# Squared distance from the row mean, one core: loads cut 3-3-2 rows, head loads and VectorE share removed

## Chip, cores and metric

One core of a Trainium2 chip. The metric is the device time in microseconds (us) of one execution. A profile's "span" is 1.7 to 1.8 us shorter than the time of its run. All runs below that are compared are in the fast state (granted clock 1.0 throughout); the single run that was not repeated is named.

## The reference

```python
x: float32, 1024 x 4096        # random normal
mean = np.mean(x, axis=-1, keepdims=True)
out  = (x - mean) ** 2         # float32, 1024 x 4096
```

16.78 MB are read and 16.78 MB written. Each of the 128 partitions of SBUF (the memory on the core) holds 8 rows of 4,096 elements; "row 3" below is the fourth row of every partition.

## The kernel before

Two tiles of four rows. Each tile's load has a small piece of 512 columns cut off ("head"), tile 0's on the SP queue (DMAs that SyncE issues), tile 1's on the ScalarE queue. VectorE makes the negated mean, ScalarE squares (x - mean) in place, and VectorE takes the last 512 columns of each tile's fourth row.

```python
for i in range(ntiles):                       # 2 tiles, Q = 4 rows, HEAD = 512
    x_tile = io.tile([P, Q * D], F32)
    if i == 0:
        nc.sync.dma_start(out=x_tile[:, :HEAD], in_=x_t[i][:, :HEAD])
        nc.sync.dma_start(out=x_tile[:, HEAD:], in_=x_t[i][:, HEAD:])
    else:
        end = Q * D - HEAD
        nc.scalar.dma_start(out=x_tile[:, end:], in_=x_t[i][:, end:])
        nc.sync.dma_start(out=x_tile[:, :end], in_=x_t[i][:, :end])
    ...
for i in range(ntiles):
    for q in range(Q):
        ...   # VectorE: neg_mean of the row (one tensor_tensor_reduce)
        cut = D if q < Q - 1 else LAST        # LAST = D - 512
        nc.scalar.activation(out=row[:, :cut], in_=row[:, :cut],
                             func=ACT.Square, bias=neg_mean, scale=1.0)
        if cut < D:
            ...   # VectorE: add neg_mean, multiply by itself, 512 columns
    nc.sync.dma_start(out=out_t[i], in_=tiles[i])
```

## Time and profile before

| | before |
|---|---|
| time, median of 3 runs | 82.99 us (82.96 to 82.99) |
| span of the profiled run | 81.4 us |
| DMA engines busy (both queues) | 96.1% of the span |
| ScalarE, VectorE busy | 36%, 26% |
| first store issued, second store issued | 39.73, 58.4 us |

A partition's share of one transfer is one piece, and each of the 16 DMA engines works through 8 pieces per transfer, one after the other. In the windows view a piece is booked where it begins, so the DMA share of a window of 1 us may be above 1. Two sums can be read from such a row. GB/s divided by share is the speed while busy. Share minus (GB/s / 434) is the time, in us of all 16 DMA engines, that the pieces begun there took beyond the plain rate of 434 GB/s. I call that the excess. The prediction shows the plain rate; the rows at the border of loads and stores, which it does not show, are these (columns: window, length, VectorE, ScalarE, GpSimd busy, clock, DMA share, GB/s):

```profile
38.00:39.00 1.00, 0.00 (x0) 1.00 (x1) 0.00 (x0) 1.00 2.05 889
39.00:40.00 1.00, 0.00 (x0) 0.71 (x1) 0.00 (x0) 1.00 0.29 127
40.00:41.00 1.00, 0.00 (x0) 0.00 (x0) 0.00 (x0) 1.00 0.15 66
41.00:42.00 1.00, 0.08 (x1) 0.00 (x0) 0.00 (x0) 1.00 2.30 983
```

889 / 2.05 = 434 for the last load pieces and 983 / 2.30 = 427 for the first store pieces: the kernel before passes from loading to storing without a loss worth the name.

### The profile page before, as it was taken

What the parts mean: (1) busy time and instruction counts of PE and PEld (TensorE: products, weight loads), DVE (VectorE), ACT (ScalarE), POOL (GpSimd) and SP (SyncE); (2) the same over time, 40 slices, a digit from 0 to 9 for tenths busy, and PEclk for the clock granted to TensorE, in tenths of its full rate; (3) what the DMA queues carried; (4) which work ended last, traced back from release to release, by engine and by line L of the source; (5) the groups of instructions that cost most, each with busy time, mean ns of one, the idle gap of its engine ahead of it and who ended that gap; (6) DMA issues with size and microseconds to landing.
All of it is one profiled execution on the core that took longest, in us unless ns stands there. A gap on an engine that the chain in (4) does not pass through costs nothing.

```text
span 81.4 us, 87 instructions
## 1 busy us (share of the span) xinstructions
DVE 20.8 (26%) x20; ACT 29.4 (36%) x9; POOL 0.2 (0%) x4
## 2 busy tenths in 40 slices
DVE  0000000000059999600039999700000000000000
ACT  0000000000054999999502999999600000000000
POOL 0000000000000000000000000000000000000000
DMA  1974999999759999995799993899996599999390
GB/s 22 704 343 187 499 499 499 499 499 437 343 218 499 499 499 499 499 406 250 343 516 515 515 515 161 354 515 515 515 516 290 258 483 515 515 515 419 161 451 0
DMA packets 864, 33.55 MB, mean 412 GB/s; under 512 B 96, under 2 KB 96, under 8 KB 352
## 3 DMA queue, kind: packets, MB, share of 16 engines
q1 hardware_dynamic: 720, 33.29, 95.0%
q10 hardware_dynamic: 144, 0.26, 1.1%
HBM read 16.78 MB, written 16.78 MB: 412 GB/s over the span
## 4 chain that ended last, share of the span: by engine, by line
DMA 49%; ACT 13%; ACTq 4%; DVE 3%; SPq 1%; issue 0%
DMA x_tile<-in_x_dram 49%; ACT x_tile L77 13%; ACTq L119 4%; DVE pairs L66 3%; SPq L53 1%; SPq L52 0%; DVE neg_mean L66 0%
## 5 line engine op out<-in xcount | busy, mean ns | idle before, releaser
L77 ACT ACTIVATE x_tile<-x_tile,neg_mean 128x4096 f32<-128x4096 f32 (+1 forms) x8 | 28.2, 3590 | 5.7 <-DVE neg_mean L66 5.7
L66 DVE CUSTOM_DVE_ANT_0 pairs<-x_tile 128x2048 f32<-128x2048 f32 x8 | 18.3, 2292 | 31.6 <-DMA x_tile<-in_x_dram 31.4
L77 ACT ACT_TABLE_LOAD x1 | 1.3, 1283 | 23.2 <-DMA x_tile<-in_x_dram 23.2
L87 DVE TENSOR_TENSOR x_tile<-x_tile 128x512 f32<-128x512 f32 x2 | 1.4, 692 | 0.1
L86 DVE TENSOR_SCALAR x_tile<-x_tile,neg_mean 128x512 f32<-128x512 f32 x2 | 1.0, 488 | 0.1
L66 DVE DVE_READ_ACCUMULATOR2_ANT neg_mean<- 128x1 f32 x8 | 0.7, 82 | 0.0
L105 POOL MEMSET const-bfloat16-1.0<- 128x1 bf16 x1 | 0.1, 102 | 0.0
L105 POOL MEMSET const-uint8-127<- 128x1 uint8 x1 | 0.1, 102 | 0.0
L105 POOL MEMSET const-float32-0.0<- 128x1 f32 x1 | 0.1, 99 | 0.2 <-issue 0.2
L105 POOL MEMSET const-float32-1.0<- 128x1 f32 x1 | 0.1, 99 | 0.0
## 6 DMA issues: line engine op xcount, KB each, us to landing
x_tile<-in_x_dram SPq DMA_DIRECT2D x2, 7936.0 KB, 31.1
x_tile<-in_x_dram ACTq DMA_DIRECT2D x1, 256.0 KB, 3.8
x_tile<-in_x_dram SPq DMA_DIRECT2D x1, 256.0 KB, 3.6
out_dram<-x_tile SPq DMA_DIRECT2D x2, 21.9
```

The source lines that it names most:

```text
L53: nc.sync.dma_start(out=x_tile[:, HEAD:], in_=x_t[i][:, HEAD:])
L66: inorder(nc.vector.tensor_tensor_reduce(out=pairs, in0=row[:, :HALF], in1=row[:, HALF:], scale=-inv_d, scalar=0.0, op0=ADD, op1=ADD, accu ...
L77: nc.scalar.activation(out=row[:, :cut], in_=row[:, :cut], func=ACT.Square, bias=neg_mean, scale=1.0,)
L86: nc.vector.tensor_scalar_add(out=rest, in0=rest, scalar1=neg_mean)
L87: nc.vector.tensor_mul(out=rest, in0=rest, in1=rest)
L105: nc = _bacc.Bacc("TRN2", target_bir_lowering=False, num_devices=1)
L119: with _tile.TileContext(nc) as tc:
```

## The change

The intent: fewer transfers and instructions, an earlier start of compute, an earlier first store. Loads of three, three and two rows, no heads, ScalarE squares whole rows, two stores of four rows. The diff is shortened. `load(lo, hi)` moves columns lo to hi of every partition's 8 rows on the SP queue, `store(first, last)` whole rows, `put(lo, hi)` stores by columns; `compute(r)` makes mean and square of row r; `inorder` keeps an instruction in program order.

```diff
-    # tiles of Q = 4 rows; heads of 512 columns on SP (tile 0) and ScalarE (tile 1)
-    nc.sync.dma_start(out=x_tile[:, :HEAD], ...)
-    nc.sync.dma_start(out=x_tile[:, HEAD:], ...)
-    nc.scalar.dma_start(out=x_tile[:, end:], ...)
-    nc.sync.dma_start(out=x_tile[:, :end], ...)
+    data = io.tile([P, ROWS * D], F32)          # one tile of 8 rows
+    load(0, 3 * D)                              # all on the SP queue
+    load(3 * D, 6 * D)
+    load(6 * D, 8 * D)
...
-            cut = D if q < Q - 1 else LAST
-            nc.scalar.activation(out=row[:, :cut], ...)
-            if cut < D:
-                nc.vector.tensor_scalar_add(out=rest, in0=rest, scalar1=neg_mean)
-                nc.vector.tensor_mul(out=rest, in0=rest, in1=rest)
-        nc.sync.dma_start(out=out_t[i], in_=tiles[i])
+        inorder(nc.scalar.activation(out=row, in_=row, func=ACT.Square, bias=neg_mean, scale=1.0))
+    for first in (0, 4):
+        for r in range(first, first + 4):
+            compute(r)
+        store(first, first + 3)
```

More of the change, by code (lines that the diff above doesn't have):

```diff
@@ L32 @@
     P = nc.NUM_PARTITIONS
-    Q = 4
-    HEAD = 512
+    ROWS = B // P
     HALF = D // 2
-    LAST = D - D // 8
-    assert B % (P * Q) == 0
-    ntiles = B // (P * Q)
+    assert B == P * ROWS and ROWS == 8
     inv_d = 1.0 / float(D)
-    x_t = x.rearrange("(p n q) d -> n p (q d)", p=P, q=Q)
-    out_t = out.rearrange("(p n q) d -> n p (q d)", p=P, q=Q)
-    io = ctx.enter_context(tc.tile_pool(name="io", bufs=ntiles))
+    x_t = x.rearrange("(p r) d -> p (r d)", p=P)
+    out_t = out.rearrange("(p r) d -> p (r d)", p=P)
@@ L45 @@
+    io = ctx.enter_context(tc.tile_pool(name="io", bufs=1))
     scratch = ctx.enter_context(tc.tile_pool(name="scratch", bufs=1))
-    stats = ctx.enter_context(tc.tile_pool(name="stats", bufs=ntiles * Q))
-    tiles = []
-    for i in range(ntiles):
-        x_tile = io.tile([P, Q * D], F32)
-        if i == 0:
-            nc.sync.dma_start(out=x_tile[:, :HEAD], in_=x_t[i][:, :HEAD])
-            nc.sync.dma_start(out=x_tile[:, HEAD:], in_=x_t[i][:, HEAD:])
-        else:
-            end = Q * D - HEAD
-            nc.scalar.dma_start(out=x_tile[:, end:], in_=x_t[i][:, end:])
-            nc.sync.dma_start(out=x_tile[:, :end], in_=x_t[i][:, :end])
-        tiles.append(x_tile)
@@ L60 @@
-    inorder = tc.keep_in_program_order
-    for i in range(ntiles):
-        for q in range(Q):
-            row = tiles[i][:, q * D:(q + 1) * D]
-            pairs = scratch.tile([P, HALF], F32)
-            neg_mean = stats.tile([P, 1], F32)
-            inorder(nc.vector.tensor_tensor_reduce(
-                out=pairs,
-                in0=row[:, :HALF],
-                in1=row[:, HALF:],
-                scale=-inv_d,
-                scalar=0.0,
-                op0=ADD,
-                op1=ADD,
-                accum_out=neg_mean,
-            ))
-            cut = D if q < Q - 1 else LAST
-            nc.scalar.activation(
-                out=row[:, :cut],
-                in_=row[:, :cut],
-                func=ACT.Square,
-                bias=neg_mean,
-                scale=1.0,
-            )
-            if cut < D:
-                rest = row[:, cut:]
-                nc.vector.tensor_scalar_add(out=rest, in0=rest, scalar1=neg_mean)
-                nc.vector.tensor_mul(out=rest, in0=rest, in1=rest)
-        nc.sync.dma_start(out=out_t[i], in_=tiles[i])
+    stats = ctx.enter_context(tc.tile_pool(name="stats", bufs=ROWS))
@@ new lines, with load, store, compute @@
+    data = io.tile([P, ROWS * D], F32)
+    inorder = tc.keep_in_program_order
+    def load(lo, hi):
+        inorder(nc.sync.dma_start(out=data[:, lo:hi], in_=x_t[:, lo:hi]))
+    def store(first, last):
+        part = slice(first * D, (last + 1) * D)
+        inorder(nc.sync.dma_start(out=out_t[:, part], in_=data[:, part]))
+    def compute(r):
+        row = data[:, r * D:(r + 1) * D]
+        pairs = scratch.tile([P, HALF], F32)
+        neg_mean = stats.tile([P, 1], F32)
+        inorder(nc.vector.tensor_tensor_reduce(
+            out=pairs,
+            in0=row[:, :HALF],
+            in1=row[:, HALF:],
+            scale=-inv_d,
+            scalar=0.0,
+            op0=ADD,
+            op1=ADD,
+            accum_out=neg_mean,
+        ))
+        inorder(nc.scalar.activation(
+            out=row, in_=row, func=ACT.Square, bias=neg_mean, scale=1.0
+        ))
```

## The prediction

> **What bounds the kernel now.** I read the page first, then the chain of waits in order of time, the timeline around the DMA issues, and the windows of one microsecond. The page says how much the engines and the transfers do:
>
> ```profile
> DVE 20.8 (26%) x20; ACT 29.4 (36%) x9; POOL 0.2 (0%) x4
> q1 hardware_dynamic: 720, 33.29, 95.0%
> q10 hardware_dynamic: 144, 0.26, 1.1%
> HBM read 16.78 MB, written 16.78 MB: 412 GB/s over the span
> ```
>
> VectorE and ScalarE are each idle for two thirds of the span of 81.4 us. The 16 DMA engines are busy for 95.0 + 1.1 = 96.1% of it, 78.2 us. Only 3.2 us are left in which an average DMA engine does nothing. So the kernel is bound by transfers, and the question for any change is which part of the 3.2 us it removes, or what it adds, or whether it makes the same bytes cost fewer DMA microseconds.
>
> The chain of waits in order of time shows where a transfer is waited for, and also misleads:
>
> ```profile
> 0.73 0.38 SPq L52
> ...
> 1.64 40.26 DMA x_tile<-in_x_dram
> ...
> 44.25 7.31 ACT x_tile L77 x2
> 51.56 3.60 ACTq L119
> 55.16 3.17 ACT x_tile L77
> ```
>
> Its second half runs through ScalarE up to 58.3 us, because it follows the second store back to the work that released it. That is not what delays the store. The timeline has both stores in one line, and the table of waits of the SP queue has how long the end waited:
>
> ```profile
> 39.73 18.97 SPq L88 DMA_DIRECT2D out_dram<-x_tile  x2
> ```
>
> ```profile
> SPq L119 <- DMA out_dram<-x_tile: 21.7, 2, 19.3
> ```
>
> The first store is issued at 39.73 us, when the loads have not yet landed (the chain has them landing at 1.64 + 40.26 = 41.90). The second is issued at 58.4 (39.73 + 18.97 is the end of its issue, 58.70). The first store's 8.39 MB cannot be through before about 60.2: see below. So each store stands in the queue before the DMA engines run out of work, and they never go dry. From the first packet to the last the queue is one unbroken stream.
>
> The windows of one microsecond give its speed. Columns: window, its length, busy time of VectorE, ScalarE and GpSimd (instructions), clock, share of 16 DMA engines' time, GB/s. A long packet is booked in the window where it begins, so shares jump above 1; GB/s divided by share is still the speed at full use:
>
> ```profile
> 2.00:3.00 1.00, 0.00 (x0) 0.00 (x0) 0.00 (x0) 1.00 0.92 236
> ...
> 8.00:9.00 1.00, 0.00 (x0) 0.00 (x0) 0.00 (x0) 1.00 2.34 1016
> ...
> 65.00:66.00 1.00, 0.00 (x0) 0.00 (x0) 0.00 (x0) 1.00 2.42 1049
> ```
>
> Loads of 15,872 columns run at 1016 / 2.34 = 434 GB/s, stores of 16,384 columns at 1049 / 2.42 = 433 GB/s, and the small head loads of 512 columns at 236 / 0.92 = 257 GB/s. The trace's packet records agree: a piece of 63,488 bytes (one partition's share of a load) takes 2.342 us on its DMA engine, one of 65,536 bytes 2.418 us, one of 2,048 bytes 84 ns at best. A line through these three is 9 ns + bytes / 27.2 GB/s.
>
> **What the Trainium skill says.** (1) "DMA: Bandwidth & Descriptors", Specifications, gives a fabric ceiling of 435 GB/s for 16 DMA engines. The trace agrees: 433 to 434 in both directions, so there is no faster rate to be had from larger pieces. (2) The same page, "Issuing engines are not separate DMA queues", says that transfers issued by several engines run on the same 16 DMA engines and interleave, and that only the issue time is saved. The trace agrees as far as it goes: the ScalarE queue (q10) moved 0.26 MB in 1.1% of the span, 0.90 us of all 16 engines, or 290 GB/s, no better than the head load on the SP queue. (3) The same page, Specifications, gives about 0.6 us to the first byte on this path. In the trace the first load is issued at 0.73 us and its first packet begins at about 1.75; I use the trace's 1.02. (4) "ScalarE: Activation LUTs", "What ACT_TABLE_LOAD costs": an ACTIVATE with a pointer bias takes about 280 ns + 0.833 ns per element, back-to-back ones overlap by 93 ns. For 4,096 columns that is 3.69 us and 3.60 from start to start; the trace has 3698 ns and the 3.60 shown above in the chain.
>
> **The change part by part.**
>
> *The 512-column loads go.* Two loads of 256 KB in 2 KB pieces, one on each queue, become part of the big ones. Bytes are the same. Per DMA engine the loads now cost 16 x 0.084 + 16 x 2.342 = 38.82 us. Afterwards each engine carries 8 pieces of 48 KB, 8 of 48 KB and 8 of 32 KB; by the line above 8 x (1.815 + 1.815 + 1.213) = 38.74 us. That saves 0.07 us. The larger part is the start: in the packet records several small packets take 0.3 to 0.6 us instead of 84 ns, on both queues, so the last of the 16 engines begins its first long packet at 4.07 us. Counted back by its 16 small packets at full speed (1.34 us) it is as if it had started at 2.73. Without the heads I expect the first packets at 1.75 to 2.0 us as now, with one such latency of about 0.45 us and not two: as if started at 2.2 to 2.45. That is 0.3 us for the engine that ends last. Saved in all about 0.35 us, on the path, as everything after it is one stream.
>
> *Heads gave no early start to compute.* The first VectorE instruction waits until 23.29 us for the whole first load, so nothing is lost there. The ACT queue's issue of 0.39 us at 0.73 also goes, in idle time.
>
> *Loads of 3, 3 and 2 rows.* 6.29 MB at 434 GB/s are 14.5 us, 4.19 MB are 9.7 us. From 2.45: the first has moved at 17.0 and lands at about 17.3 (in the trace landings follow the last packet by 0.3 to 0.4 us), the second at 31.8, the third at 41.5 (now 41.9). Compute on rows 0 to 2 runs from 17.3.
>
> *One ACTIVATE per row, and no VectorE rest.* VectorE loses 2 x (0.49 + 0.69) = 2.4 us, ScalarE gains two times 512 columns x 0.83 ns = 0.9 us. Both lie beside the transfers. For the stores: rows 0 to 2 end on ScalarE at 17.3 + 2.3 (mean of row 0; the table load of 1.28 runs beside it) + 3 x 3.6 = 30.4. Row 3 waits for the second load: 31.8 + 2.3 + 3.7 = 37.8, and the first store is issued at about 37.9, against 39.73 now. Rows 4 and 5 follow to 45.0, rows 6 and 7 (in SBUF at 41.5, means by 46.2) to 52.3, and the second store is issued at 52.4 against 58.4 now.
>
> *Stores.* Same size and count as before. A store issued at 37.9 has its first packet ready about 1.0 us later, at 38.9; the loads occupy the DMA engines to about 41.2. So 2.3 us to spare. The first store then runs 8 x 2.418 = 19.3 us to 60.5, and the second has been waiting for 8 us by then. No gap in either place, and as none exists now, none is removed.
>
> *Sum.* DMA work 38.74 + 38.69 = 77.43 us from 2.45: 79.9 us; last landing 80.2; the span's tail after it (80.6 to 81.4 now) stays: 81.0 us instead of 81.4. The time before is 82.99, so 82.99 - 0.35 = 82.64, or 82.65 us, 0.4% less.
>
> **The rivals.** *First, the queue goes dry at a store.* If the first store came later than about 40.2 us, each microsecond more would be a microsecond of idle DMA. For it: the store of four rows needs row 3, which comes only with the second load, and the path behind that landing is serial (2.3 + 3.7 us). Against it: the 2.3 us to spare. It needs ScalarE to lag by more than half a row. It would make the time 83 to 85 us.
>
> *Second, the earlier start of compute is worth something.* Compute starts 6 us earlier and the last store is issued 6 us earlier; by the chain of waits one would say that the time falls by 6 us, to 77. Against it: the second store would only stand in the queue for longer. 33.55 MB at 434 GB/s take 77.3 us whatever the order, and 77.3 + 2.2 before and 1.1 after are all of 80.6. I give this almost nothing.
>
> *Third, the heads were a help.* Small first packets might bring all 16 engines to work sooner than packets of 48 KB, and the 3-way cut costs 8 more pieces of 32 to 48 KB. Then the gain at the start is nil or turns into a loss: 82.9 to 83.1 us. The many slow small packets in the records speak against it.
>
> **Range and chances.** The step that is least sure is the 0.3 us of the start; from nil to 0.6 is possible, with 0.07 for the pieces, and a small chance of a gap at the first store. That gives 82.25 to 83.05. Two per cent would be 1.66 us: a gain of that size is more than half of the 3.2 us in which the DMA engines are idle at all, and a loss needs a store that is 4 us later than reckoned. So within 2% with 0.96, faster 0.02, slower 0.02.
>
> **What would show each step.** The DMA queue part should show one queue alone, with about 95 to 96% of a span of 81.0 us; the first row mean at 17.3 us; stores issued at about 37.9 and 52.4; no window with idle DMA between 2.5 and 79 us; ScalarE 30.3 us busy, VectorE 19. The prediction is wrong if the stream shows a hole between loads and stores, if the rate of 48 KB pieces is not 434 GB/s, or if the first packets begin later than 2.0 us.

## The result

| | before, same rounds | changed |
|---|---|---|
| time, median of 4 runs | 82.97 us (82.86 to 82.99) | 83.83 us (83.69 to 83.94) |
| ratio | | 1.0106 (95%: 1.0091 to 1.0121) |
| span of the profiled run | 81.4 us | 81.9 us |

A ratio here is the mean time of one kernel's fast runs over that of the other's of the same rounds, so it is not quite the ratio of the medians. The change is slower by 1%, within 2% of before as forecast, but the direction is wrong and the time lies outside the range of 82.25 to 83.05 us.

The page of the changed kernel, parts 1 and 3:

```profile
DVE 18.4 (22%) x16; ACT 30.3 (37%) x9; POOL 0.2 (0%) x4
q1 hardware_dynamic: 720, 33.55, 96.1%
HBM read 16.78 MB, written 16.78 MB: 410 GB/s over the span
```

The DMA engines are as busy as before, 96.1%, but of a longer span: 78.7 us instead of 78.2 for the same bytes. So nothing went idle; some bytes became dearer. Its timeline, with the first VectorE instruction after each load and the stores:

```profile
17.62 2.29 DVE L57 CUSTOM_DVE_ANT_0 pairs<-data 128x2048 f32<-128x2048 f32 x1 [17.62 <-DMA data<-in_x_dram]
...
32.26 2.29 DVE L57 CUSTOM_DVE_ANT_0 pairs<-data 128x2048 f32<-128x2048 f32 x1 [7.67 <-DMA data<-in_x_dram]
...
38.33 14.74 SPq L51 DMA_DIRECT2D out_dram<-data  x2
...
42.55 2.29 DVE L57 CUSTOM_DVE_ANT_0 pairs<-data 128x2048 f32<-128x2048 f32 x1 [3.33 <-DMA data<-in_x_dram]
```

The first two loads are in use at 17.62 and 32.26 us, 14.64 us apart; the prediction had 14.5. The third is in use 10.29 us after the second, where its 4.19 MB at 434 GB/s take 9.7. About 0.6 us are lost inside the third load. The windows show where:

```profile
38.00:39.00 1.00, 1.00 (x1) 1.00 (x2) 0.00 (x0) 1.00 1.22 492
39.00:40.00 1.00, 0.23 (x2) 1.00 (x1) 0.00 (x0) 1.00 0.51 164
40.00:41.00 1.00, 0.00 (x0) 1.00 (x1) 0.00 (x0) 1.00 1.28 393
41.00:42.00 1.00, 0.00 (x0) 1.00 (x2) 0.00 (x0) 1.00 2.12 918
```

In the first three rows, the last load pieces, the speed is 403, 322 and 307 GB/s, and in the fourth, the first store pieces, 433. The excess is (1.22 - 492/434) + (0.51 - 164/434) + (1.28 - 393/434) = 0.09 + 0.13 + 0.37 = 0.59 us. In the packet records the last 32 KB piece of each DMA engine takes 1.54 to 1.87 us and the one before it 1.21 to 1.46, where earlier ones take 1.213. The first store was issued at 38.33 us; by the 1.0 us that the prediction took from the trace, its packets stood ready from about 39.35, an estimate. The slow pieces are those under way after that moment.

### The profile page after: what moved, and what is told of

Read it like the earlier page. It is cut to its first block, busy times and chain, and to the rows that moved or that the text cites. A ratio compares the mean times of both kernels' runs of the same rounds, so it can differ in the third digit from the quotient of the medians.

```text
span 81.9 us, 81 instructions
## 1 busy us (share of the span) xinstructions
DVE 18.4 (22%) x16; ACT 30.3 (37%) x9; POOL 0.2 (0%) x4
## 3 DMA queue, kind: packets, MB, share of 16 engines
q1 hardware_dynamic: 720, 33.55, 96.1%
## 4 chain that ended last, share of the span: by engine, by line
DMA 38%; ACT 14%; ACTq 4%; issue 4%; DVE 3%; SPq 0%; DVEq 0%
DMA data<-in_x_dram 38%; ACT data L67 14%; ACTq L108 4%; DVE pairs L57 3%; SPq L47 0%; DVEq L57 0%; DVE neg_mean L57 0%
## 5 line engine op out<-in xcount | busy, mean ns | idle before, releaser
L67 ACT ACTIVATE data<-data,neg_mean 128x4096 f32<-128x4096 f32 x8 | 29.0, 3697 | 4.7 <-DVE neg_mean L57 4.7
L57 DVE CUSTOM_DVE_ANT_0 pairs<-data 128x2048 f32<-128x2048 f32 x8 | 18.3, 2292 | 28.8 <-DMA data<-in_x_dram 28.6
```

The lines of the kernel that those rows point to most:

```text
L57: inorder(nc.vector.tensor_tensor_reduce(out=pairs, in0=row[:, :HALF], in1=row[:, HALF:], scale=-inv_d, scalar=0.0, op0=ADD, op1=ADD, accu ...
L67: inorder(nc.scalar.activation(out=row, in_=row, func=ACT.Square, bias=neg_mean, scale=1.0))
```

## The experiments

Theory Q: a store that stands ready while loads are still under way makes the last load pieces slow, and the time is lost for good; the change brought this about by issuing the first store earlier. Rivals: the missing heads cost the time (H), ScalarE's whole rows do (A), or the cut 3-3-2 with its 32 KB pieces. The diffs are shortened, and lines in plain words stand for DMA calls. Ratios are to the kernel before, in the same rounds and on the same chip; medians of before were 83.06, 83.03, 83.12 and 83.17 us in the four groups of runs. "Excess at the border" is that of the load pieces near the first store, from the packet records as in the sum above.

### Two loads instead of three

```diff
-    load(0, 3 * D); load(3 * D, 6 * D); load(6 * D, 8 * D)
+    load(0, 4 * D); load(4 * D, 8 * D)
```

> The changed kernel with two loads of four rows instead of three loads of 3, 3 and 2 rows; everything else as changed. Theory Q (a store that stands in the queue while a load is still being written slows the load's last pieces, 0.6 us here): the first store is issued at about 39.7 us again, just as the loads end, so the last load pieces keep 2.42 us each and the time is 82.6 to 83.0 us (before 82.97), about 0.9 below the changed kernel's 83.83. Theory H (the missing 512-column heads cost the time): no heads here either, so 83.6 to 83.9 us. Theory A (one ACTIVATE per whole row, ScalarE 0.9 us longer): also 83.6 to 83.9.

83.09 us, ratio 1.0005 (0.9991 to 1.0020). The first store is issued at 39.37 us, the excess at the border is nil. Theory A falls, and so does H as the sole cause: no heads and whole rows, yet the time of before.

### The changed kernel, first store held back by 1.8 us

```diff
+    square(3, m3, 0, D - 512)
+    square(4, m4, 0, K)          # K = 1344, ahead of the end of row 3
+    square(3, m3, D - 512, D)
     store(0, 3)
+    square(4, m4, K, D)
```

> The changed kernel, three loads as they are, but ScalarE squares the first 1,344 columns of row 4 ahead of the last 512 columns of row 3, so that the first store is issued about 1.5 us later, at 39.8 instead of 38.3 us. Theory Q: the store's packets are ready at about 40.9, as the loads end (40.9 to 41.3), the last load pieces go back to 1.21 us, and the time falls by 0.4 to 0.9 us to 82.9 to 83.4. If the cost lies in the three loads or their 32 KB pieces themselves, or in the missing heads: no change, 83.7 to 83.9, and the last load pieces stay at 1.5 to 1.9 us. If later is only later: 83.8 to 85.

83.44 us, ratio 1.0046 (1.0033 to 1.0060). The store was issued at 40.10 us, later than meant; the load pieces are all plain, so the three loads and their sizes are not what is slow. Only half of the loss came back, a little less than theory Q expected. In this profile the DMA engines stood idle for 0.16 us between loads and store, as the store was now late, and the first pieces of the kernel cost an excess of 0.94 us, the most of any profile. The next runs left open how much a well placed store would bring.

### The kernel before, with half of its first store issued early, and a control

```diff
             if i == 0 and q == 1:                       # early: after rows 0, 1
+                store rows 0 and 1 of tile 0
-        store tile i
+        store rows 2 and 3 of tile 0 (then tile 1 as a whole)
```

The control has the same two halves, rows 2 and 3 first, rows 0 and 1 right after, both at the end.

> The kernel before with its first store cut in two of two rows each, the first of them issued as soon as rows 0 and 1 are squared, at about 33 us, some 8 us before the loads end. Theory Q with a fixed cost at the border of loads and stores: 0.5 to 0.9 us more than the same cut with both halves issued at the end (the run beside this one), about 83.6 to 84.0 us. Theory Q with a cost in proportion to the time in the queue (0.6 us in 2 us here): 2 to 3 us more. If an early store costs nothing: same as the run beside it, 83.0 to 83.2.

> The control for the run with the early half store: the kernel before with its first store cut into the same two halves, rows 2 and 3 issued first and rows 0 and 1 right after, so that both are issued at about 39.7 us as the loads end. The cut alone costs 8 pieces more per DMA engine, 0.07 us, and one more issue that is hidden: 83.0 to 83.1 us by all theories.

Early: 84.43 us, ratio 1.0160 (1.0147 to 1.0173). Control: 83.13 us, ratio 1.0003 (0.9991 to 1.0016). The two kernels differ only in when and in which order the halves are stored, and the early one takes 1.3 us longer. Windows of the early one:

```profile
36.00:37.00 1.00, 0.00 (x0) 1.00 (x2) 0.00 (x0) 1.00 2.34 1016
37.00:38.00 1.00, 0.00 (x0) 1.00 (x1) 0.00 (x0) 1.00 0.00 0
38.00:39.00 1.00, 0.00 (x0) 1.00 (x1) 0.00 (x0) 1.00 3.81 1016
```

The last load piece of every DMA engine (begun after 38 us) takes 3.81 us in the mean for the bytes that took 2.34 in the round before: an excess of 1.47 us. The store was issued at 32.66 us and so, by the same 1.0 us, ready since about 33.7, and the rounds before are untouched. So this is a lump at the border, not a cost for each microsecond in the queue.

### Which store, and does the size of the last load pieces matter?

```diff
 # only one early store: rows 2 and 3 follow after the first row of tile 1
+            if i == 1 and q == 0: store rows 2 and 3 of tile 0
```

> The kernel before with rows 0 and 1 stored early, at about 33 us, as in the run with the early half store (84.43 us; there the last load piece of every DMA engine, and it alone, took 3.6 to 4.2 us instead of 2.34), but with rows 2 and 3 stored only after the first row of the second tile is squared, at about 48 us, long after the loads. If the one store that stands next in the queue stretches the last load piece: again 3.6 to 4.2 us for that piece and about 84.4 us in all. If it was the issue of the second half store at 39.4 us, in the middle of that piece: 2.34 us and 83.1 us.

84.50 us, ratio 1.0182 (1.0167 to 1.0197); the program had the second half's issue at 39.67 all the same, since nothing in the data held it back, so the run repeats the one above (excess 1.50 us) and does not separate the two stores. The measurements without compute, below, do.

```diff
 # last 512 columns of the last big load as a load of their own, in the early kernel (first) ...
-    load tile 1, 15,872 columns
+    load tile 1, 15,360 columns; then 512 columns
 # ... and in the changed kernel (second)
-    load(6 * D, 8 * D)
+    load(6 * D, 8 * D - 512); load(8 * D - 512, 8 * D)
```

> The run with the early half store again (84.43 us), but the second tile's load is cut so that its last 512 columns come as a load of their own at the end: the last load piece of each DMA engine is then 2 KB instead of 62 KB. Theory P (only the last load piece, the one just ahead of the store, is slowed, by some six tenths of its own time): the excess falls from 1.47 us to about 0.1 and the time to 83.1 to 83.3 us. Theory F (a fixed amount at the border, set by the store or by time): 84.4 us as before, with several small pieces slowed.

> The changed kernel with its last load cut into 7,680 and 512 columns, so that the last load pieces are 2 KB each; all else, and the early first store at 38.3 us, as changed (1.0106 times before). Theory P: most of the 0.6 us of slow last pieces goes, 83.2 to 83.5 us, ratio 1.002 to 1.006. Theory F: 83.8 to 83.9 us, ratio 1.010.

84.41 us, ratio 1.0168 (1.0150 to 1.0186), and 84.11 us, ratio 1.0128 (1.0108 to 1.0147). My theory P falls: with 2 KB pieces last, the 60 KB pieces ahead of them take the excess (1.24 of 1.40 us), and in the changed kernel the 30 KB ones (0.67 us in their last round). The lump is not removed by cutting the last load. The second run was even slower than theory F expected (83.8 to 83.9 us); that is not explained.

### A head put back into the changed kernel

```diff
-    load(0, 3 * D)
+    load(0, 512); load(512, 3 * D)
```

> The changed kernel with one 512-column head put back ahead of its first load, on the same queue; the slow border at the first store stays. In the profiles so far the first pieces cost the mean DMA engine 0.33 to 0.59 us above the plain rate with the heads (four profiles with two heads) and 0.62 to 0.94 us without. If heads help at the start: ratio to before 1.006 to 1.009 instead of 1.0106, 83.5 to 83.8 us. If they do not, as the prediction had it: 1.0106 or more, since 8 more pieces per DMA engine cost 0.07 us.

83.86 us, ratio 1.0098 (1.0083 to 1.0113), not to be told from 1.0106. The head did nothing measurable; the border's excess was there (0.80 us in this profile, the store being issued at 38.27 us).

### Raw stores: no compute at the border

Rows 0 to 3 are stored as loaded, straight after the first load, so that nothing but DMA works until the loads end. Their outputs are wrong, which doesn't matter for the times.

```diff
+    load(0, 4 * D); load(4 * D, 8 * D)
+    for lo, hi in zip(cuts, cuts[1:]): put(lo, hi)     # raw, at 22.6 us
+    for r in range(4, 8): compute(r)
+    put(4 * D, 8 * D)
 # cuts = (0, 4D)  |  (0, D, 2D, 3D, 4D)  |  (0, 512, 4D)
```

> A measurement, wrong on purpose: two loads of four rows; rows 0 to 3 are stored as loaded, without mean or square, in one store issued as soon as they land, at about 22.5 us, 19 us before the second load ends; rows 4 to 7 are computed and stored as in the changed kernel. No engine but DMA works until the loads end. Theory S (the cost is the first store piece's own length, handled alongside the last load pieces, when it stands ready early enough): its first piece is 64 KB, 2.4 us, so the last load pieces lose about 2.4 us, 85.2 us in all. Theory C (a fixed cost of about 1.4 us once the store is early enough): 84.4 us. If the cost comes from ScalarE or VectorE working at the border and not from the queue: none here, 82.9 to 83.1 us.

> The same measurement with the first store cut into four of one row each, all issued at about 22.5 to 24 us: the first store piece of each DMA engine is 16 KB, 0.6 us. Theory S: 0.6 us lost at the border, plus 0.22 us for 24 more pieces per DMA engine, 83.6 to 83.8 us. Theory C: 1.4 us lost, 84.5 us.

> The same measurement with the first store cut into 512 columns and 15,872 columns, both issued at about 22.5 us: the first store piece is 2 KB, 0.084 us. Theory S in its narrow form: 0.1 us lost, 83.1 us. If several pieces of the store are taken ahead of their turn, the cost follows bytes and not pieces: 1.4 us or more, 84.4 us and up.

84.32, 84.52 and 84.33 us; ratios 1.0146, 1.0166 and 1.0147 (intervals of less than 0.002 to either side). The windows of the first:

```profile
36.00:37.00 1.00, 0.00 (x0) 0.00 (x0) 0.00 (x0) 1.00 2.42 1049
...
38.00:39.00 1.00, 0.00 (x0) 0.00 (x0) 0.00 (x0) 1.00 2.40 721
39.00:40.00 1.00, 0.00 (x0) 0.00 (x0) 0.00 (x0) 1.00 1.05 328
```

VectorE and ScalarE columns are zero, and still 1049 / 2.42 = 433 GB/s falls to 721 / 2.40 = 300 in the last round of load pieces. The excess is 1.03, 1.26 and 1.02 us for first store pieces of 64, 16 and 2 KB. So the engines that compute have no part in it, and theory S (the first store piece's own length) falls too: 2 KB or 64 KB, the lump is the same. Why the 16 KB run has 0.2 us more is not explained.

### The changed kernel with a small first store piece

```diff
-    store(0, 3)
+    put(4 * D - 512, 4 * D); put(0, 4 * D - 512)
```

> The changed kernel with its first store cut into the last 512 columns of row 3, stored first, and the rest; both are issued at about 38.3 us, as the changed kernel's first store is. Theory S: the loss at the border, 0.6 us, falls to 0.1 and the time to 83.2 to 83.5 us (ratio 1.003 to 1.006). Theory C: 83.8 to 84.0 us, ratio 1.010 to 1.012.

83.71 us, ratio 1.0069 (1.0048 to 1.0089), border excess 0.51 us. That is a little above what S expected, and the interval also meets that of the unaltered changed kernel in the next group. The border's excess is still there, so the small piece did not do what S says.

### How early is early? Three kernels in one job

The changed kernel with K = 640 instead of 1,344; the changed kernel with rows 0 to 2 stored as soon as they are squared; the changed kernel unaltered.

```diff
-    K = 1344          # held back 1.8 us
+    K = 640           # held back 1.1 us
 # and, in the changed kernel:
             compute(r)
+            if r == 2: store(0, 2)
-        store(first, first + 3)
+        store(3 if first == 0 else 4, first + 3)
```

> The changed kernel with its first store held back less than in the first such run: 640 columns of row 4 instead of 1,344 ahead of the end of row 3, so it is issued at about 39.5 us (changed 38.3, the late store 40.1, where the DMA engines stood idle for 0.16 us). If the loss grows with how early the store is issued (0 at about 39.7, 0.6 at 38.3): 0.0 to 0.2 us lost at the border, no idle DMA, ratio to before 1.002 to 1.005, 83.2 to 83.45 us. If any store issued before the loads end costs the same: 0.6 us and ratio 1.010.

> The changed kernel with its first store cut into rows 0 to 2, issued as soon as they are squared at about 30.9 us, 10 us before the loads end, and row 3 at 38.3 us as now. If the changed kernel's 0.6 us is a part of the lump of 1.0 to 1.45 us that very early stores cost: that whole lump here, ratio 1.014 to 1.019, 84.2 to 84.6 us. If the 0.6 us is something of its own that the 38.3 us issue causes: 1.010 or 1.020 and more.

> The changed kernel once more, unaltered, on the same chip as these runs: ratio 1.009 to 1.012, 83.7 to 83.95 us, with 0.4 to 0.8 us lost in the last two load pieces of each DMA engine and 0.6 to 0.9 us in the first pieces.

| kernel | first store issued | excess at border | time | ratio (95%) |
|---|---|---|---|---|
| held back 1.1 us | 39.44 us | 0.00 us | 83.16 us | 0.9995 (0.9977 to 1.0013) |
| changed | 38.41 us | 0.47 us | 83.85 us | 1.0086 (1.0065 to 1.0106) |
| rows 0 to 2 early | 30.98 us | 1.07 us | 84.35 us | 1.0138 (1.0119 to 1.0157) |

Holding the first store back by 1.03 us (39.44 against 38.41) makes the changed kernel 0.69 us faster, and brings it to the time of before. The held-back kernel's windows at the border, for comparison with the changed kernel's above:

```profile
38.00:39.00 1.00, 1.00 (x1) 1.00 (x3) 0.00 (x0) 1.00 0.91 393
39.00:40.00 1.00, 0.43 (x2) 1.00 (x2) 0.00 (x0) 1.00 0.61 262
40.00:41.00 1.00, 0.00 (x0) 1.00 (x1) 0.00 (x0) 1.00 0.99 426
41.00:42.00 1.00, 0.00 (x0) 1.00 (x1) 0.00 (x0) 1.00 2.43 1049
```

432, 430, 430 and 432 GB/s: nothing slow, and no gap, though ScalarE is busy throughout. Its third load is used from 42.17 us on, instead of 42.55 and 42.66 in the two profiles of the changed kernel:

```profile
39.44 0.35 SPq L51 DMA_DIRECT2D out_dram<-data  x1
42.17 2.29 DVE L57 CUSTOM_DVE_ANT_0 pairs<-data 128x2048 f32<-128x2048 f32 x1 [2.75 <-DMA data<-in_x_dram]
```

### The same raw store on the other queue

```diff
-        put(lo, hi)                                   # SP queue, behind the load
+        inorder(nc.scalar.dma_start(out=out_t[:, lo:hi], in_=data[:, lo:hi]))
```

> A measurement, wrong on purpose: as the raw early store in one piece of 64 KB per partition, but issued on the ScalarE queue, so that the store and the second load share every DMA engine in turn from about 23.7 us on. 2 x 8.39 MB at 434 GB/s are 38.7 us: if loads and stores in flight together cost nothing, the second load lands at about 58 to 60.5 us, pieces pass at 2.4 us each, and the whole takes about 98 us (rows 4 to 7 are computed and stored after it). If each change from load to store piece costs about 1.0 to 1.4 us (8 changes per DMA engine), the load lands at about 68 to 72 us and the whole takes 107 to 111 us.

99.93 us (one run, state unknown; 98 was expected if the mixture is free). The second load landed at 59.71 us, within the 58 to 60.5 expected for that case. The windows:

```profile
24.00:25.00 1.00, 0.00 (x0) 0.00 (x0) 0.00 (x0) 1.00 3.27 1049
...
27.00:28.00 1.00, 0.00 (x0) 0.00 (x0) 0.00 (x0) 1.00 2.42 1049
...
32.00:33.00 1.00, 0.00 (x0) 0.00 (x0) 0.00 (x0) 1.00 2.42 1049
...
34.00:35.00 1.00, 0.00 (x0) 0.00 (x0) 0.00 (x0) 1.00 1.66 721
```

The store was issued at 22.71 us. The load pieces under way a microsecond later still take 2.42 us; the next ones, begun at 24.05 to 24.77 and just ahead of the first store pieces, are slow: 1049 / 3.27 = 321 GB/s, an excess of 0.85 us. From there each DMA engine takes one store piece and one load piece in turn, 8 store pieces and the 7 load pieces that are left, and every one passes at 2.42 us, 433 GB/s. That the two queues' pieces interleave on the same DMA engines is what the Trainium skill says ("DMA: Bandwidth & Descriptors", "Issuing engines are not separate DMA queues"). So, as far as one run shows, it is neither loads and stores in flight together nor each change between them that costs: the lump is paid once, at the first store that is ready while loads run.

## Why the prediction was wrong

- **Bound by transfers, one unbroken stream: right.** The DMA engines are 96.1% busy before and after, no gap opened, and 2.4 us less on VectorE and 0.9 us more on ScalarE changed nothing (the two-load kernel has both and a ratio of 1.0005). The second rival, a gain from earlier compute, got nothing, as said.
- **Landings and issues: right within 0.5 us, but for the last.** First load in use 17.62 (17.3 predicted), second 32.26 (31.8 and its landing), stores at 38.33 and 52.72 (37.9 and 52.4; 38.33 + 14.74 is the end of the second issue, which takes 0.35). The third load's data were in use at 42.55 (41.5 predicted for the landing): 0.6 us of that is more than its bytes explain.
- **The step that failed first: "So 2.3 us to spare. (...) No gap in either place".** No gap came, as it said. What failed is the cost that it gave to a waiting store: it treated a store that waits in the queue as free, kept the last load pieces at the plain rate (the 38.74 us of its sum), and looked only for a store that comes too late. The runs show the opposite hazard. At 39.37 to 39.73 us the issue costs nothing (the two-load, held-back, control and before kernels), at 38.3 to 38.4 it costs 0.47 to 0.80 us of DMA time (0.59 and 0.47 in the two profiles of the changed kernel, 0.51 to 0.80 in its three variants), and from 33 us and earlier 1.0 to 1.5 us in the same queue. In time, this is the 0.69 us between the changed kernel and its held-back form.
- **The step that failed second: 0.3 us saved at the start without the heads.** By the prediction's own measure (the DMA engine that starts its long pieces last, counted back), the changed kernel is as if started at 2.75 and 2.84 us in its two profiles, not at 2.45; before had 2.73, and the four other profiles with two heads 2.47 to 2.67. The ten other profiles without heads have 2.78 to 3.04. The first pieces carry an excess without heads too, and not a smaller one: in the changed kernel's first profile 49,152 bytes took 2.18 to 2.65 us instead of 1.815, and two of the 16 DMA engines began only at 2.16 and 2.38 us, one of the signs of being wrong that the prediction had named ("later than 2.0 us"). The third rival ("the gain at the start is nil or turns into a loss") was right about the start, though not about the size of the loss (82.9 to 83.1 us in all); in times, removing the heads is worth nothing either way (1.0005 with two loads, 0.9995 held back, 1.0098 with a head against 1.0086 and 1.0106 without).
- **The sum.** Predicted -0.35 us, of which 0.07 was for fewer pieces. Measured +0.86 us in the first job and +0.7 in the last. A start that saves nothing and the border's 0.69 us give +0.6; the rest of the first job's figure is not explained by its profile, whose run was the fastest of the four. Two slips in the prediction change nothing: the head load's 257 GB/s comes from a window that holds both queues' heads, so it cannot show that the ScalarE queue is "no better"; and 20.8 - 2.4 makes VectorE 18.4 us busy, as measured, and not 19.

**What stays open** is the mechanism of the lump inside the DMA engine. It is not the length of the pieces on either side, not compute, not the mixture of directions as such, and it is paid once. With a store issued 8 us and more before the border, the excess sits in the last 64 KB or so of each DMA engine's load bytes (the last two 32 KB pieces with rows 0 to 2 early, the last 64 KB piece in the raw runs). That the engine already works on the store's first bytes then would fit, but it is a guess: no run here looks inside an engine. Why the lump is 1.0 us in some runs and 1.5 in others is open too. Whether the first 2 KB or the whole queue of store pieces has to be waiting was not separated either.

No version here beats the kernel before. The changed kernel with its store held back equals the kernel before.

## What to carry to other kernels

In a kernel bound by transfers, total DMA microseconds decide, so compare them (busy share times span), not only gaps: a change that leaves no gap can still make bytes dearer. Where a queue passes from loads to stores, look at when the first store is issued. Here it was free 1.4 to 1.9 us before the DMA engines ended their last load pieces (issued at 39.37 to 39.73 us; mean end, from the packet records, 41.1 to 41.4). Earlier cost up to 1.5 us once. The store at 40.10 us, about 1.4 us before the end of its loads, already left the engines idle for 0.16 us, so that is the edge. And when a tuned kernel has a store issued "just in time", suspect that this is part of its tuning before moving it.

## What the Trainium skill lacked or had wrong

- "DMA: Bandwidth & Descriptors", Rules for kernel authors, advises issuing a DMA early and waiting on its semaphore late. The page gives no cost for a store that is ready while loads are under way: 0.47 to 0.80 us for a store issued at 38.3 to 38.4 us, 0.85 to 1.50 us for one issued at 33 us or earlier, none at 39.37 to 39.73.
- The same page, Specifications, gives about 0.6 us to the first byte on this path. It does not say from which moment. Here the first packet began 1.02 us after the issue began (0.73 to 1.75 us), which is 0.64 us after the issue ended (0.73 + 0.38 = 1.11), so the figure agrees only when counted from the end. Nor does it say that the first pieces are slow: of 49,152 bytes they took 2.18 to 2.65 us instead of the plain 1.815.
